# Eight experts in an order ranked on the chip, with weights loaded by register and a kind for 32 tokens

## The chip, the core and the metric

The kernel runs on one core of one Trainium2 chip. The metric is the device time of one execution in microseconds (us), as a median over runs. A profile is one further execution: its span runs from its first instruction to its last.

## The reference

Two layers of a decoder trunk over 256 tokens of width 1024: a token mixer (attention beside a state-space branch), then a channel mixer, which is a dense SwiGLU in layer 0 and eight SwiGLU experts in layer 1. All weights are 32-bit floats. Each token goes to the two experts with the highest router logits:

```python
logits = (t @ w_router + b_router).astype(jnp.float32)
top_val, top_idx = lax.top_k(logits, TOP_K)          # TOP_K = 2 of N_EXPERTS = 8
top_w = jax.nn.softmax(top_val, axis=-1)
gates = jnp.sum(jax.nn.one_hot(top_idx, N_EXPERTS) * top_w[..., None], axis=1)
out = jnp.zeros_like(t)
for e in range(N_EXPERTS):
    out = out + gates[:, e:e + 1] * (jax.nn.silu(t @ w1[e]) * (t @ w3[e])) @ w2[e]
```

The experts' outputs are summed, so their order is free. With the inputs used here the router gives experts 0 to 7 this many tokens: 20, 54, 194, 113, 23, 40, 43, 25. One expert's three matrices (1024 x 2816, twice, and 2816 x 1024) hold 34.6 MB.

## The kernel before

Everything up to the last expert layer stays as it is and is not told here. `moe_begin` (L1078) starts the expert layer while the mixer of layer 1 still runs: it lists the weights of all experts in the order of their use as pieces of 1 MiB (`parts`, L1084: 33 pieces an expert, 22 for the two first matrices and 11 for the last one) and sets up a **ring** of 15 buffers of 1 MiB. `refill` (L178) issues, on SP's DMA queue, the load of the next pieces as far as the ring has room; each load waits for the release of its buffer.

`route` (L1021) computes the logits, the two best experts of a token, the number of tokens of each expert and each token's rank in its expert, and from the counts, on VectorE, a number `ov` for each expert (L1049 to L1051): how many of 64, 128 and 208 the count exceeds. The loop over the experts (L1417) loads that number into a register of all five engines and branches by it (L1426 to L1435). Each expert therefore stands in the program four times, as four **kinds**: `small` for up to 64 tokens, `middle` up to 128, `many` up to 208 and `many` for all 256. Of the four, one runs, and the other three are jumped over. They stand in the program in this order: small, middle, many(208), many(256); small follows the branch directly.

- `small` (L1168) gathers the expert's tokens with a matrix product by a 0/1 matrix (L1175), transposes them (L1183), and runs 11 steps. In a step, `stage1` multiplies the tokens by 512 columns of the first two matrices (L1200), and `stage2` transposes the product of the step before (L1212) and adds its share of the output (L1218). The tokens stand in TensorE as stationary weights of 64 columns; a matrix product is cut into two halves that use two column groups of the array (`tile_position=(0, 64 * h)`) at the same time. The weights come straight from the ring as 32-bit floats. At the end the output is scaled by the gates (L1234) and scattered back over the tokens by another matrix product (L1240), and VectorE adds it to the stream x_t (L1141).
- `middle` (L1245) and `many` (L1316) first split every weight into two parts of a faster format on ScalarE and VectorE (L210, L211) and run three matrix products in place of one.

With the counts above the kinds in order are: small, small, many(208), middle, small, small, small, small. In the tables of the trace "PE" is TensorE, "PEld" its weight loads, DVE VectorE, ACT ScalarE, and a 32-bit matrix product makes two records.

Of the kernel before, what the change touches and what calls it, by code (L numbers as in the profile page):

```python
# [46 lines left out]
MANY = 208  # L47
ENGS = [mybir.EngineType.PE, mybir.EngineType.Activation, mybir.EngineType.DVE, mybir.EngineType.SP,
# [43 lines left out]
def trunk_kernel(ctx: ExitStack, tc: tile.TileContext, xT, sm, co, w_ada0, w_ada, w_in, w_v, s5bc, w_glu,  # L92
# [83 lines left out]
    ring, parts, turn, filled = [], [], [0], [0]  # L176
# [844 lines left out]
    def route(mo, hn, a, sh, b2, xp, lgp, ss, _):  # L1021
# [26 lines left out]
        ov, o64 = tl("ov", [8], I32), lg[:, 0, :]  # L1048
        V.tensor_scalar(o64, ps[:, 16:24], 64.0, None, op0=ALU.is_gt)  # L1049
        V.scalar_tensor_tensor(o64, ps[:, 16:24], float(P), o64, op0=ALU.is_gt, op1=ALU.add)  # L1050
# [8 lines left out]
        return y, rk, ov, (m8, o0, o1)  # L1059
# [18 lines left out]
    def moe_begin():  # L1078
# [6 lines left out]
        for e in range(NE):  # L1085
            for j in range(NB + 1):
                if j < NB:
                    parts.extend((w13m[e, j, :, 4 * i:4 * i + 4, :], 4) for i in range(2))
                if j:
                    parts.append((w2m[e, j - 1], 2))  # L1090
# [7 lines left out]
    def moe():  # L1098
        mo, hn = rt[1]
        sh = rt[0][1]  # L1100
        y0, rk, ov, picks = route(mo, hn, *rt[0])
# [3 lines left out]
        def ahead(e):  # L1105

            if e == 0:
                gates_of(mo, gates, *picks)
            if e < NE - 1:
                slots_of(e + 1)  # L1110
# [5 lines left out]
        def slots_of(e):  # L1116
# [21 lines left out]
        slots_of(0)  # L1138
# [29 lines left out]
        def small(e):  # L1168

            pm = pms[e % 2]  # L1170
            hf = (slice(0, 64), slice(64, 128))
            ps = [mm_ps("xg") for _ in range(2)]
            for tb in range(2):
                for h in range(2):
                    PE.matmul(ps[h][hf[h], :], lhsT=pm[:, tb, 0:64], rhs=hn[:, tb, 512 * h:512 * h + 512],  # L1175
                              start=tb == 0, stop=tb == 1, tile_position=(0, 64 * h))
            xs = mo.tile([P, 512], F32, name=nm("xs"), tag="pt", bufs=2)
            S.activation(xs[hf[0]], ps[0][hf[0], :], AF.Copy)
            V.tensor_copy(xs[hf[1]], ps[1][hf[1], :])
            ps = mm_ps("xg")  # L1180
            xe = lp.tile([P, KC * 64], F32, name=nm("xs"), tag="hh")
            for c in range(4):
                PE.transpose(ps[:, c * P:(c + 1) * P], xs[:, c * P:(c + 1) * P], ident)  # L1183

            xe4, ps4 = (t.rearrange("p (c h s) -> p h c s", c=4, h=2) for t in (xe, ps))
            for h in range(2):
                V.tensor_tensor(xe4[:, h], ps4[:, h], sh[:, 4 * h:4 * h + 4].unsqueeze(2).broadcast_to([P, 4, 64]), op=ALU.add)  # L1187
            y = [ms_ps("y", 0) for _ in range(2)]

            def rows_of(src, rows, cols):  # L1190
                n = min(rows, 2048 // cols)
                return [w[:, r, :] for i in range(0, rows, n)
                        for w in (load_raw(src[:, i:i + n, :], n, cols),) for r in range(n)]

            def stage1(j):
                w = rows_of(w13m[e, j], KC, 512)
                ps = [mm_ps("s1") for _ in range(2)]
                for k in range(KC):
                    for h in range(2):
# [3 lines left out]
                sg = mo.tile([P, 256], F32, name=nm("sg"), tag="pt", bufs=2)  # L1203
# [410 lines left out]
```

## Time and profile before

| what | value |
| --- | --- |
| median of 3 runs (lowest, highest) | 1573.48 us (1571.73, 1580.18) |
| the profiled execution's own time | 1569.24 us |
| its span | 1567.5 us |
| PE busy in the span | 1371.7 us (88%) |
| DVE, ACT, POOL busy | 881.6, 605.2, 318.9 us |
| moved by DMA | 420.37 MB, 268 GB/s over the span |
| chain of waits that ended last | PE 70%, DVE 18%, issue 6% |

The own time is that of the execution with the profile; the span leaves out what lies before the first and after the last instruction. The busy shares are means over stages with different limits: the first 740 us are the two mixers and the dense channel mixer, the rest is the expert layer, and there the share of a single stretch says more than the mean.

### The profile page before, as it was taken

The numbers are of one execution on the slowest core, as the hardware profiler recorded it, in microseconds if no ns is written. First come the engines' busy times: TensorE is split into PE (matmuls) and PEld (weight loads), VectorE is DVE, ScalarE is ACT, GpSimd is POOL, SyncE is SP. The second block draws the span as 40 slices with busy tenths as digits, with TensorE's granted clock in tenths as the row PEclk, the third lists the DMA queues.
The fourth block names the chain that finished last, engine by engine and source line by source line (L and its number), as shares of the span: only waits on it lengthen the run. The fifth ranks groups of instructions, "written<-read, shape, count | busy, mean of one in ns | idle before, by whom it ended". The sixth has DMA issues, their size and how long they took to land.

```text
span 1567.5 us, 24755 instructions
## 1 busy us (share of the span) xinstructions
PE 1371.7 (88%) x9903; PEld 1139.8 (73%) x9903; DVE 881.6 (56%) x1443; ACT 605.2 (39%) x1115; POOL 318.9 (20%) x295
## 2 busy tenths in 40 slices
PE   4788999799998878988998949999799897979796
PEld 3676998699997777988665648988677574747474
DVE  7888679897777778687111036666588301010102
ACT  3453564354455534644111125555477211111112
POOL 0568019986201625050000000000000000000000
PEclk8898999799999899999998969999899998989899
DMA  7454356477776344479899975666399599999993
GB/s 285 174 190 160 125 188 212 136 258 240 261 257 223 133 136 135 166 244 403 359 419 416 419 290 189 215 203 203 130 348 351 212 420 416 419 416 419 417 419 122
DMA packets 60379, 420.37 MB, mean 268 GB/s; under 512 B 6688, under 2 KB 6688, under 8 KB 11296
## 3 DMA queue, kind: packets, MB, share of 16 engines
q1 hardware_dynamic: 56160, 403.34, 67.9%
q0 software_dynamic: 4032, 14.68, 2.8%
q8 instruction: 100, 1.64, 0.4%
q14 instruction: 87, 0.71, 0.1%
HBM read 416.94 MB, written 1.05 MB: 267 GB/s over the span
## 4 chain that ended last, share of the span: by engine, by line
PE 70%; DVE 18%; issue 6%; DMA 2%; ACT 2%; DVEq 0%; SPq 0%; ACTq 0%
PE s L1200 16%; PE mm L231 15%; PE y L1218 8%; DVE wl L211 6%; PE s L1350 4%; PE y L1372 4%; PE facc L971 3%; PE s L1267 3%; PE s L1352 2%; PE y L1286 2%; DMA raw<-in_w13m_dram 2%; DVE acc L309 1%; PE mm L716 1%; PE xg L1175 1%; DVE x_t L1141 1%
## 5 line engine op out<-in xcount | busy, mean ns | idle before, releaser
L211 DVE TENSOR_TENSOR wl<-raw,wh 128x1024 fp32r<-128x1024 f32 (+1 forms) x290 | 391.0, 1363 | 118.6 <-ACT wh L210 116.2
L210 ACT ACTIVATE wh<-raw 128x1024 fp32r<-128x1024 f32 (+1 forms) x290 | 302.3, 1057 | 252.1 <-PE mm L231 102.1
L231 PE MATMUL mm<-hh,wh 128*128 128x256 f32 x864 | 250.7, 292 | 5.1 <-ACT hh L250 2.9
L231 PE MATMUL mm<-hh,wl 128*128 128x256 f32 x864 | 249.7, 290 | 5.8 <-DVE wl L211 5.8
L1200 PE MATMUL s<-raw,xs 128*64 128x256 f32 x1920 | 250.1, 390 | 3.4 <-DVE xs L1187 3.4
L231 PE MATMUL mm<-hl,wh 128*128 128x256 f32 x864 | 249.5, 289 | 2.0 <-DVE hl L251 1.0
L1200 PEld LDWEIGHTS s<-raw,xs 128*64 128x64 f32 x1920 | 183.8, 140 | 48.2 <-issue 13.9
L1205 DVE TENSOR_TENSOR sg<-sg,s 64x256 f32<-64x256 f32 x66 | 28.0, 424 | 318.6 <-ACT sg L1204 269.8
L231 PEld LDWEIGHTS mm<-hh,wl 128*128 128x128 f32 x864 | 169.4, 196 | 9.8 <-DVE wl L211 6.3
L231 PEld LDWEIGHTS mm<-hh,wh 128*128 128x128 f32 x864 | 169.0, 196 | 9.4 <-ACT hh L250 3.3
L231 PEld LDWEIGHTS mm<-hl,wh 128*128 128x128 f32 x864 | 169.2, 196 | 3.7 <-DVE hl L409 1.5
L1218 PE MATMUL y<-raw,gT 128*64 128x512 f32 x520 | 143.1, 600 | 4.7 <-ACT gT L1215 4.7
L1204 ACT ACTIVATE sg<-s 64x256 f32<-64x256 f32 x66 | 24.8, 375 | 314.2 <-PE s L1200 314.2
L1350 PE MATMUL s<-xe,wh 128*128 128x416 f32 x352 | 107.2, 368 | 2.0 <-DVE sg L1360 1.7
L1352 PE MATMUL s<-xe,wl 128*128 128x208 f32 x352 | 91.0, 258 | 0.0
L309 DVE SCALAR_TENSOR_TENSOR acc<-raw,cond,acc 128x512 f32<-128x512 f32 x91 | 81.4, 894 | 1.6
L1218 PEld LDWEIGHTS y<-raw,gT 128*64 128x64 f32 x520 | 51.1, 136 | 40.9 <-issue 30.5
L317 POOL TENSOR_TENSOR araw<-araw,cond 128x1024 f32<-128x1024 f32 x28 | 62.3, 2229 | 71.8 <-DMA araw<-in_w_ada_dram 71.8
L1350 PEld LDWEIGHTS s<-xe,wh 128*128 128x128 f32 x352 | 66.2, 188 | 4.3 <-DVE sg L1360 2.4
L1352 PEld LDWEIGHTS s<-xe,wl 128*128 128x128 f32 x352 | 67.3, 191 | 0.4
L971 PE MATMUL facc<-fgh,wh 128*128 128x256 f32 x352 | 62.9, 281 | 0.2 <-ACT wh L210 0.2
L321 POOL TENSOR_TENSOR araw<-araw,araw 128x1024 f32<-128x1024 f32 x21 | 58.2, 2773 | 1.6
(513 smaller groups left out, 2369.0 us busy)
## 6 DMA issues: line engine op xcount, KB each, us to landing
raw<-in_w13m_dram SPq DMA_DIRECT2D x160, 1024.0 KB, 13.8
raw<-in_w2m_dram SPq DMA_DIRECT2D x87, 1024.0 KB, 13.7
raw<-in_w_ada_dram SPq DMA_DIRECT2D x32, 1024.0 KB, 5.1
raw<-in_w_in_dram SPq DMA_DIRECT2D x28, 1024.0 KB, 5.0
raw<-in_w13d_dram SPq DMA_DIRECT2D x22, 1024.0 KB, 5.0
late<-in_w13m_dram SPq DMA_DIRECT2D x16, 1024.0 KB, 16.2
araw<-in_w_ada_dram POOLq DMA_DIRECT2D x28, 512.0 KB, 4.6
raw<-in_w2d_dram SPq DMA_DIRECT2D x11, 1024.0 KB, 5.0
```

Source lines behind the costliest of these rows:

```text
L210: S.activation(hv, rv, AF.Copy)
L211: V.tensor_tensor(lv, rv, hv.bitcast(F32), op=ALU.subtract)
L231: PE.matmul(ps, lhsT=a[k][:, c0:c0 + P], rhs=b[:, k, :], start=k == 0 and i == 0 and o % 2 == 0, stop=k == n - 1 and i == 2 and o % 2 == 1)
L309: V.scalar_tensor_tensor(acc0, raw[:, k, :], c, acc0, op0=ALU.mult, op1=ALU.add)
L317: G.tensor_tensor(raw, raw, cond[:, r0:r0 + 2].unsqueeze(2).broadcast_to([P, 2, 512]), op=ALU.mult)
L321: G.tensor_tensor(acc, acc, raw, op=ALU.add)
L971: PE.matmul(o, lhsT=a[k][:, oc * P:(oc + 1) * P], rhs=b[:, k, :], start=j == 0 and oc % 2 == 0 and k == 0 and i == 0, stop=j == NB - 1 and ...
L1200: PE.matmul(ps[h][hf[h], 0:256], lhsT=xe4[:, k // 4, k % 4, :], rhs=w[k][:, 256 * h:256 * h + 256], start=k == 0, stop=k == KC - 1, tile_p ...
L1218: PE.matmul(y[h][hf[h], :], lhsT=g[:, k, :], rhs=w[k][:, 512 * h:512 * h + 512], start=j == 0 and k == 0, stop=j == NB - 1 and k == 1, til ...
L1350: PE.matmul(ps[:, 0:2 * nb], lhsT=hs[k][:, c], rhs=x.rearrange("p i s -> p (i s)"), start=k == 0, stop=False)
L1352: PE.matmul(ps[:, nb:2 * nb], lhsT=ls[k][:, c], rhs=x[:, 0, :], start=False, stop=k == KC - 1)
L1372: PE.matmul(y[b][n][0:s1 - s0, :], lhsT=g[:, k, s0:s1], rhs=w[w_][k][:, n * 512:n * 512 + 512], start=j == 0 and k == 0 and i == 0, stop=j ...
```

## The change

Expert 0 stays first. Experts 1 to 7 are ranked by their number of tokens on the chip (`ordered`), and position i of 1 to 7 gets the expert of rank PLACE[i-1], rank 0 having most tokens. `place` is a new row of constants; `bring` picks a row's values into the new order by a sum over a 0/1 matrix. The ranks `rk`, the gates and the kinds are brought into this order, and the expert of each position is loaded into a register of SP, from which the addresses of its weights are made. `small` takes its number of rows n as an argument (32 or 64), and cuts each product into 128/n column groups; its two halves' results now share one PSUM tile. The branches are nested so that the heavy kinds follow directly and the small ones are jumped to.

With the counts above positions 0 to 7 hold experts 0, 2, 7, 3, 5, 1, 6, 4, and their kinds are small(32), many(208), small(32), middle, small(64), small(64), small(64), small(32).

```diff
+PLACE = (0, 5, 1, 4, 2, 3, 6)
     def refill():
         while filled[0] < min(len(parts), turn[0] + len(ring)):
-            src, rows = parts[filled[0]]
+            w, e, (j, i), rows = parts[filled[0]]
+            if e and not experts:
+                return
+            src = w[0, j] if e == 0 else w[bass.ds(experts[e - 1], 1), j].squeeze(0)
+            if i is not None:
+                src = src[:, 4 * i:4 * i + 4, :]
...
-        V.tensor_scalar(o64, ps[:, 16:24], 64.0, None, op0=ALU.is_gt)
-        V.scalar_tensor_tensor(o64, ps[:, 16:24], float(P), o64, op0=ALU.is_gt, op1=ALU.add)
+        V.tensor_scalar(o64, ps[:, 16:24], 32.0, None, op0=ALU.is_gt)
+        for n in (64, P):
+            V.scalar_tensor_tensor(o64, ps[:, 16:24], float(n), o64, op0=ALU.is_gt, op1=ALU.add)
+        key = tl("key", [8])
+        V.scalar_tensor_tensor(key, ps[:, 16:24], 8.0, cov('iota8'), op0=ALU.mult, op1=ALU.subtract)
+    def ordered(mo, key, ov, rk):
+        above, rank, ow, seq = tl("above", [8, 8]), tl("rank", [8]), tl("ow", [8, 8]), tl("seq", [2, 8])
+        V.tensor_tensor(above[:, 0:7, 0:7], key[:, 1:8].unsqueeze(1).broadcast_to([P, 7, 7]),
+                        key[:, 1:8].unsqueeze(2).broadcast_to([P, 7, 7]), op=ALU.is_gt)
+        V.memset(rank[:, 0:1], -1.0)
+        V.reduce_sum(rank[:, 1:8], above[:, 0:7, 0:7], axis=AX.X)
+        V.tensor_tensor(ow, rank.unsqueeze(1).broadcast_to([P, 8, 8]), cov('place').unsqueeze(2).broadcast_to([P, 8, 8]),
+                        op=ALU.is_equal)
+        def bring(o, row):
+            V.tensor_tensor(above, ow, row.unsqueeze(1).broadcast_to([P, 8, 8]), op=ALU.mult)
+            V.reduce_sum(o, above, axis=AX.X)
+        bring(seq[:, 0, :], cov('iota8'))
+        bring(seq[:, 1, :], ov)
+        si = tl("si", [2, 8], I32)
+        V.tensor_copy(si, seq)
+        for tb in range(2):
+            bring(seq[:, tb, :], rk[:, tb, :])
+        return bring, si, seq
...
+        for e in range(1, NE):
+            experts.append(nc.values_load(si[0:1, 0, e:e + 1], engines=[mybir.EngineType.SP], min_val=0, max_val=NE - 1,
...
-        def small(e):
+        def small(e, n):
+            G_ = P // n
+            cb = KC // G_
+            gr = [slice(n * g, n * g + n) for g in range(G_)]
...
+                c_ = 512 // G_
                 for k in range(KC):
-                    for h in range(2):
-                        PE.matmul(ps[h][hf[h], 0:256], lhsT=xe4[:, k // 4, k % 4, :], rhs=w[k][:, 256 * h:256 * h + 256],
-                                  start=k == 0, stop=k == KC - 1, tile_position=(0, 64 * h))
+                    for g in range(G_):
+                        PE.matmul(ps[gr[g], 0:c_], lhsT=xe4[:, k // cb, k % cb, :], rhs=w[k][:, c_ * g:c_ * g + c_],
+                                  start=k == 0, stop=k == KC - 1, tile_position=(0, n * g))
...
-            for h in range(2):
-                S.activation(ys[hf[h]], y[h][hf[h], :], AF.Copy, scale=gs[hf[h]])
+            S.activation(ys, y[:, 0:w_], AF.Copy, scale=gs)
...
-            rv = nc.values_load(ov[0:1, e:e + 1], engines=ENGS, min_val=0, max_val=3,
+            rv = nc.values_load(si[0:1, 1, e:e + 1], engines=ENGS, min_val=0, max_val=4,
...
-            with tc.If(rv < 1) as c:
-                arm(small)
+            with tc.If(rv < 2, preferred_fallthrough_block=False) as c:
+                with tc.If(rv < 1, preferred_fallthrough_block=False) as c1:
+                    arm(lambda e: small(e, 32))
+                with c1.Else():
+                    arm(lambda e: small(e, 64))
             with c.Else():
-                with tc.If(rv < 2) as c2:
+                with tc.If(rv < 3, preferred_fallthrough_block=False) as c2:
                     arm(middle)
                 with c2.Else():
-                    with tc.If(rv < 3) as c3:
+                    with tc.If(rv < 4) as c3:
                         arm(lambda e: many(e, MANY))
```

Three places show how instructions move (a number behind a name is that of the buffer).

**TensorE at the second position: which kind follows the branch.** Before, the branch rows of the second position, each with the first row behind it (L1175 is `small`, L1254 `middle`, L1333 `many`):

```order
L1418 TENSOR_LOAD rov_7908
L1426 COMPARE_AND_BRANCH
L1175 MATMUL xg_12670<-late,pm_7921 64x512
...
L1426 UNCONDITIONAL_BRANCH
L1429 COMPARE_AND_BRANCH
L1254 MATMUL xg_13096<-pm_7921,late 128x128 x8
...
L1429 UNCONDITIONAL_BRANCH
L1432 COMPARE_AND_BRANCH
L1333 MATMUL xg_13981<-pm_7921,late 128x128 x2
```

Now (L1382 is `many`, L1223 `small`, with 64 rows first and with 32 rows behind it, L1303 `middle`):

```order
L1467 TENSOR_LOAD rsi_7939
L1476 COMPARE_AND_BRANCH
L1482 COMPARE_AND_BRANCH
L1485 COMPARE_AND_BRANCH
L1382 MATMUL xg_15304<-pm_7924,late 128x128 x2
...
L1485 UNCONDITIONAL_BRANCH
L1477 COMPARE_AND_BRANCH
L1223 MATMUL xg_14007<-late,pm_7924 64x512 x4
...
L1477 UNCONDITIONAL_BRANCH
L1223 MATMUL xg_13376<-late,pm_7924 32x256 x8
...
L1477 UNCONDITIONAL_BRANCH
L1303 MATMUL xg_14419<-pm_7924,late 128x128 x8
```

Where `small` followed its branch directly, `many` for 208 tokens now does. A small(64) is reached by one taken branch (over `many`), a small(32) by two (over `many`, then over small(64)), a `middle` by one. Each kind but the last in the program ends with a branch behind all of them, before and now.

**TensorE in one step of the kind for 32 rows** (L1250 is `stage1`, L1263 the transpose and L1268 the product of `stage2`):

```order
L1263 MATMUL gT_13598<-co_t,sg_13544 128x64
L1250 MATMUL s_1952_13611<-late,xe_13389 32x128 x5
L1268 MATMUL y_13396<-raw_7663,gT_13600 32x256 x8
L1250 MATMUL s_1952_13611<-late,xe_13389 32x128 x11
L1250 MATMUL s_1952_13611<-raw_7650,xe_13389 32x128 x16
```

A step has 32 products of 128 columns and 8 of 256, where `small` before has 16 of 256 and 4 of 512: twice as many, half as long, and four of them side by side in the array where two were.

**VectorE between the counts and the branch's value.** These rows stand between the last comparison of the counts (L1059) and the load of the kind (L1467):

```order
L1059 SCALAR_TENSOR_TENSOR rov_7908<-rank_7902,rlg_7885 128x8
L1062 TENSOR_TENSOR rrk_7913<-rank_7902,roh_7898 128x16
L1065 SCALAR_TENSOR_TENSOR rkey_7916<-rank_7902,co_t 128x8
L1063 TENSOR_SCALAR rrk_7913<-rrk_7913 128x16
L1079 TENSOR_TENSOR rabove_7927<-rkey_7916 128x7x7
L1158 TENSOR_SCALAR pm_7923<-co_t,rrk_7913 128x128 x2
L1082 TENSOR_REDUCE rrank_7928<-rabove_7927 128x7
L1084 TENSOR_TENSOR row_7929<-rrank_7928,co_t 128x64
L1088 TENSOR_TENSOR rabove_7927<-row_7929,co_t 128x64
L1089 TENSOR_REDUCE rseq_7930<-rabove_7927 128x8
L1088 TENSOR_TENSOR rabove_7927<-row_7929,rov_7908 128x64
```

One more sum (L1089) and the cast to whole numbers (L1093) follow, and then the branch's value is there; before, L1051 gave it directly.

## Rows read from the trace of the kernel before

**Rows 1.** Window: busy us of PE, PEld, DVE, ACT, POOL; granted clock, DMA share, GB/s.

```profile
1396.00:1479.00 83.00, 73.44 (x510) 48.12 (x508) 9.63 (x23) 9.51 (x26) 0.00 (x0) 0.93 1.01 418
```

**Rows 2.** Timeline of PE, one step: start us, us, engine, line, operation, tiles, shapes, count.

```profile
1455.18 0.34 PE L1212 MATMUL gT<-co_t,sg 64*128 64x64 f32 x2
1457.72 3.18 PE L1200 MATMUL s<-raw,xs 128*64 128x256 f32 x26
1460.84 0.34 PE L1212 MATMUL gT<-co_t,sg 64*128 64x64 f32 x2
```

**Rows 3.** Timeline of PE, a small expert's first and last products; idle time before in brackets.

```profile
1394.20 3.68 PE L1175 MATMUL xg<-late,pm 128*64 128x512 f32 x8 [5.95 <-issue]
1466.93 3.22 PE L1240 MATMUL sc<-ge,ys 64*128 64x256 f32 x16 [0.77 <-ACT ys L1234]
1476.51 3.68 PE L1175 MATMUL xg<-late,pm 128*64 128x512 f32 x8 [6.35 <-issue]
```

**Rows 4.** Timeline of PE, sixteen narrow products; then their line's row, ns min/median/max.

```profile
499.18 0.54 PE L672 MATMUL kps<-vt,bp 128*32 128x96 f32 x16
L672 PE MATMUL kps<-vt,bp x128: 245/246/271, 156.1 to 501.0; 128*32 128x96 f32 x128
```

**Rows 5.** DMA issues of 1 MiB: count, KB, median us from issue to landing.

```profile
raw<-in_w13d_dram SPq DMA_DIRECT2D x22, 1024.0 KB, 5.0
```

**Rows 6.** Refill at a start: SP's DMA issue; busy time by window (as rows 1).

```profile
1239.96 0.33 SPq L183 DMA_DIRECT2D raw<-in_w13m_dram  x1
1233.00:1239.00 6.00, 4.55 (x22) 1.77 (x20) 1.45 (x3) 0.59 (x1) 0.00 (x0) 0.77 0.00 0
```

**Rows 7.** Timeline of PE and ACT, end of the last expert.

```profile
1546.38 1.94 PE L1218 MATMUL y<-raw,gT 128*64 128x512 f32 x8 [0.43 <-ACT gT L1215]
1548.34 1.39 ACT L1234 ACTIVATE ys<-y,gs 64x512 f32<-64x512 f32 x2 [2.02 <-PE y L1218]
```

**Rows 8.** Timeline, first row of a kind, idle time before it in brackets; last row DVE.

```profile
924.14 1.19 PE L1333 MATMUL xg<-pm,late 128*128 128x128 f32 x4 [20.70 <-issue]
1117.75 6.37 PE L1254 MATMUL xg<-pm,late 128*128 128x128 f32 x32 [6.87 <-DVE wl L211]
1232.22 3.60 PE L1175 MATMUL xg<-late,pm 128*64 128x512 f32 x8 [3.63 <-issue]
917.74 0.48 DVE L1119 TENSOR_SCALAR pm<-co_t,rrk 128x128 f32<-128x128 f32 x2 [13.42 <-issue]
```

**Rows 9.** PE's branches: line, queue, count, ns min/median/max, start us.

```profile
L1426 PEldq COMPARE_BRANCH  x1: 95/95/95, 744.4 to 744.4; - x1
L1426 PEldq COMPARE_BRANCH  x1: 6138/6138/6138, 820.5 to 820.5; - x1
L1426 PEldq COMPARE_BRANCH  x1: 7179/7179/7179, 909.1 to 909.1; - x1
L1429 PEldq COMPARE_BRANCH  x1: 7396/7396/7396, 916.5 to 916.5; - x1
L1426 PEldq COMPARE_BRANCH  x1: 4356/4356/4356, 1113.1 to 1113.1; - x1
L1429 PEldq COMPARE_BRANCH  x1: 3958/3958/3958, 1227.5 to 1227.5; - x1
```

**Rows 10.** Busy time by window around branches (columns as rows 1).

```profile
744.00:752.00 8.00, 4.84 (x16) 1.79 (x18) 5.19 (x28) 1.87 (x2) 0.00 (x0) 0.71 0.94 388
902.00:924.00 22.00, 1.32 (x8) 0.64 (x6) 4.49 (x12) 2.95 (x3) 0.00 (x0) 0.56 0.97 382
1107.00:1117.00 10.00, 3.87 (x30) 3.67 (x30) 7.40 (x15) 4.79 (x6) 0.00 (x0) 0.79 0.04 8
1227.00:1232.00 5.00, 1.59 (x14) 1.38 (x12) 3.70 (x9) 0.00 (x0) 0.00 (x0) 1.00 0.03 7
```

**Rows 11.** Timeline of DVE and PE at the start of the experts.

```profile
743.35 0.17 DVE L1051 SCALAR_TENSOR_TENSOR rov<-rank,rlg 128x8 int32<-128x8 f32 x1
744.69 3.39 PE L1175 MATMUL xg<-late,pm 128*64 128x512 f32 x8 [1.77 <-DMA raw<-in_w13m_dram]
```

More of the change, by code (lines that the diff above doesn't have):

```diff
@@ L173, in wtile @@
             i -= b
-    ring, parts, turn, filled = [], [], [0], [0]
+    ring, parts, experts, turn, filled = [], [], [], [0], [0]
     def refill():
         while filled[0] < min(len(parts), turn[0] + len(ring)):
-            src, rows = parts[filled[0]]
+            w, e, (j, i), rows = parts[filled[0]]
[4 more added lines that the diff above has]
+                src = src[:, 4 * i:4 * i + 4, :]
             b = ring[filled[0] % len(ring)].rearrange("p (r c) -> p r c", r=rows)
@@ L1087, in moe_begin @@
                 if j < NB:
-                    parts.extend((w13m[e, j, :, 4 * i:4 * i + 4, :], 4) for i in range(2))
+                    parts.extend((w13m, e, (j, i), 4) for i in range(2))
                 if j:
-                    parts.append((w2m[e, j - 1], 2))
+                    parts.append((w2m, e, (j - 1, None), 2))
         ring.extend([rp.tile([P, 2048], F32, name=nm("raw"), tag="raw", bufs=MR) for _ in range(MR)])
@@ L1100, in moe @@
         sh = rt[0][1]
-        y0, rk, ov, picks = route(mo, hn, *rt[0])
+        y0, rk0, ov, key, picks = route(mo, hn, *rt[0])
         gates = mo.tile([P, 2, 8], F32, name="gates")
@@ L1108, in ahead, with slots_of @@
                 gates_of(mo, gates, *picks)
+                for tb in range(2):
+                    bring(gates[:, tb, :], gates[:, tb, :])
             if e < NE - 1:
-                slots_of(e + 1)
+                slots_of(e + 1, rk)
         gt2 = ada_v(1, 5)
         pms = [mo.tile([P, 2, P], F32, name=f"pm{i}") for i in range(2)]
-        def slots_of(e):
+        def slots_of(e, rk):
             for tb in range(2):
@@ L1136, in back_of @@
             return ge, gs
-        slots_of(0)
+        slots_of(0, rk0)
+        bring, si, rk = ordered(mo, key, ov, rk0)
+        for e in range(1, NE):
+            experts.append(nc.values_load(si[0:1, 0, e:e + 1], engines=[mybir.EngineType.SP], min_val=0, max_val=NE - 1,
+                                          skip_runtime_bounds_check_because="it is a sum over a one-hot row"))
         def add_back(e, ch, y):
@@ L1188, in small @@
-            y = [ms_ps("y", 0) for _ in range(2)]
+            xe4, ps4 = (t[:, 0:KC * n].rearrange("p (c g s) -> p g c s", c=cb, g=G_) for t in (xe, ps))
+            for g in range(G_):
+                V.tensor_tensor(xe4[:, g], ps4[:, g], sh[:, cb * g:cb * g + cb].unsqueeze(2).broadcast_to([P, cb, n]),
+                                op=ALU.add)
+            y = ms_ps("y", 0)
             def rows_of(src, rows, cols):
-                n = min(rows, 2048 // cols)
-                return [w[:, r, :] for i in range(0, rows, n)
-                        for w in (load_raw(src[:, i:i + n, :], n, cols),) for r in range(n)]
+                m = min(rows, 2048 // cols)
+                return [w[:, r, :] for i in range(0, rows, m)
+                        for w in (load_raw(src[:, i:i + m, :], m, cols),) for r in range(m)]
@@ L1417, in moe @@
         for e in range(NE):
-            rv = nc.values_load(ov[0:1, e:e + 1], engines=ENGS, min_val=0, max_val=3,
-                                skip_runtime_bounds_check_because="it is a sum of three comparisons")
+            rv = nc.values_load(si[0:1, 1, e:e + 1], engines=ENGS, min_val=0, max_val=4,
+                                skip_runtime_bounds_check_because="it is a sum of four comparisons")
             def arm(f):
@@ L1561, in pack @@
     puc('iota8', np.broadcast_to(np.arange(8, dtype=f32)[None], (P, 8)))
+    puc('place', np.broadcast_to(np.array((-1,) + PLACE, dtype=f32)[None], (P, 8)))
     puc('iota128', np.broadcast_to(np.arange(P, dtype=f32)[None], (P, P)))
```

75 lines of the change are left out of this document (37 added, 38 removed).

## The prediction

> **What bounds the kernel now.** I read the busy time by window first. Over one period of a light expert near the end, PE is busy for 73 of 83 us while the DMA engines are at a share of 1.01 and move 418 GB/s [rows 1]: both are near their limit. 1 MiB at 418 GB/s is 2.51 us, so the 33 blocks of an expert need 82.8 us. The timeline of PE says which of the two leads. Between two transposes of `stage2` lie 1460.84 - 1455.18 = 5.66 us, one of eleven steps, with no row that waits for a DMA [rows 2]. A step takes three blocks, 7.53 us of DMA; the ring of 15 blocks pays the difference, and is filled again in the idle time between the experts, so it is not PE that waits. A light expert is bound by PE: from its first product (1394.20) to the end of its last (1466.93 + 3.22 = 1470.15) it takes 75.95 us, and then PE idles for 6.35 us until the next [rows 3]. That idle time is the second thing to read: 3.63 to 6.87 us ahead of most experts, but 20.70 us ahead of the third [rows 8]. PE's branch records fill it: a branch that is not taken lasts 95 ns, a taken one 4 to 7.4 us [rows 9].
>
> **The kind for 32 tokens.** It runs at positions 0, 2 and 7. The nearest row for its products: sixteen records of 96 columns with 32-wide weights, spread over four column groups by L672, take 0.54 us, and one alone 0.246 us [rows 4], so one adds (0.54 - 0.246)/15 = 20 ns. With two groups, 26 records of 256 columns take 3.18 us [rows 2], about 0.38 us for the first and 112 ns for each further one; that is 224 ns for 256 columns on one group, or 84 ns for 96. The 20 ns are a quarter of it: four groups do work at once. So each group's columns are halved, and of a step's 5.66 us the products, some 5 us, shrink to 2.5: a step of about 3.2 us. [...] The expert's time follows from the ring. Before, SP issued its first refill 1239.96 - 1232.22 = 7.7 us after the first product, and DMA stood still until then [rows 6]; with shorter first products I take 5.7 to 6.1 us. A block lands 5.0 us after an issue on an empty queue [rows 5], and block 33 is the 18th to be fetched: 6 + 5 + 17 x 2.51 = 53.6 us. Behind it come its products (1.3), the scaling (0.4) and the scatter (3.2, as in rows 3), 4.9 us: 58.5 us instead of 75.95. Two such experts give -34.9. The last one ends with the work that follows it: its last product of `stage2` ended at 1546.38 + 1.94 = 1548.32 of a span of 1567.5 [rows 7], 19.2 us ahead of the end. Before, from 1476.51 to the end, 91.0 us; now 53.6 + 1.3 + 0.2 + 18.9 = 74.0: -17.0. Bounds for each: 62 (a release later by 3 us) and 55 (the first block of the next expert issued earlier).
>
> **The kind for 64 tokens** keeps its products; at its end one operation on ACT replaces two that took 1.39 us [rows 7], -0.7 each, three times -2.1. `many` and `middle` are unchanged but for their place, 0; both take longer than 82.8 us, so a ring that a light expert left empty fills beside them. That is the cover of this zero: if it fails, `middle` waits for its first blocks, at most 5.0 us.
>
> Experts together: **-34.9 - 17.0 - 2.1 = -54.0 us**.
>
> **The jumps between experts.** Every kind ends with one taken branch, before and now. What changes are the branches ahead of a kind: before 0 for `small`, 1 for `middle`, 2 for `many`; now 0 for `many`, 1 for small(64) and `middle`, 2 for small(32). Prices: the first, at the end of an expert, is in the gaps (5.95 to 6.35 in rows 3, a record of 6.14 in rows 9, with the DMA engines full). One further jump cost 7.18 and 7.40 us with DMA at 0.97, and 4.36 and 3.96 where DMA was at 0.04 and 0.03 [rows 9, 10]; I take 7.3 and 4.2. Which price holds is read from the kind that ends: `many` and `middle` leave the ring full and DMA still; the light kinds leave blocks queued (33 released in 75 us, at most 30 landed). In order:
>
> - 0 to 1 (`many`): 6.1, as before.
> - 1 to 2 (small(32)), behind `many`: 6.87 with two taken [rows 8], one more, 11.0.
> - 2 to 3 (`middle`): 5.95 + 7.3 = 13.3.
> - 3 to 4 (small(64)), behind `middle`: 3.63 [rows 8] + 4.2 = 7.8.
> - 4 to 5 and 5 to 6: 13.3 each.
> - 6 to 7 (small(32)): three taken, as in the 20.70 of before, 20.7.
>
> Sum 85.5. Before, in order: 6.1 + 20.7 + 6.87 + 3.63 + 5.95 + 5.95 + 6.35 = 55.5 (rows 3 and 8; one 5.95 stands for two). **+30.0 us**.
>
> [...]
>
> **The start.** Before, the branch's value was there at 743.35 + 0.17 = 743.52 and the first product ran at 744.69 [rows 11]. Now a dozen operations on VectorE stand ahead of it, each 0.17 to 0.28 us: +2.6 at the end of the chain. Then two jumps ahead of small(32) on PE, while DMA is still at 0.94 [rows 10]: 6.0 and, the ring being full by then, 4.2. First product at 757.5 instead of 744.7: **+12.8**, between +7 (both jumps hidden behind the chain in part) and +17.5 (both full price). SP also loads seven registers and adds one operation per DMA. No row shows that; the nearest is SP's spacing of issues, 2.51 us each, so I take 0, and up to 1 us for the loads.
>
> **Sum against the profiled execution**: -54.0 + 30.0 + 12.8 = -11.2, its own time 1569.24 becomes 1558.0; the median shown is 4.2 us above that execution, so 1562. The prices move it: with 62 or 55 us for a small(32) it is +10 or -10, so the likeliest case alone spans 1552 to 1572.
>
> **Rivals.**
>
> *B, jumps at the low price.* An extra jump costs what it does without DMA traffic, 4 us, and a first one 3.63. For it: behind `middle` the ring is full, and light experts with longer gaps need blocks at less than the rate that DMA has (75 + 13 = 88 us against 82.8). Against it: at the end of each light expert some 7 blocks are still queued: 33 are released, and 65/2.51 = 26 land, since the first takes 10 us. Gaps 7 x 3.63 + 8 x 4.2 = 59, +3.5; start +10.8; sum -39.7: 1534.
>
> *C, jumps at the full price everywhere, slower.* Let q be the price of every further jump. Eight of them stand between experts and one more at the start; with 5.95 for each first one the growth is 9q - 5.2. At q = 7.3 it is 60.5, net +6.5, 1580; at 8.0, near the 13.42 us that VectorE idled over two jumps and more [rows 8], net +12.8, 1586. It decides for slower than the old time from q = 6.6. For it: all seven prices measured while DMA was full are 6 to 7.4. Against it: behind `many` and `middle` DMA stands at 0.03 and 0.04 [rows 10].
>
> [...]
>
> *E, the kind for 32 does not gain*, because its four groups run one behind the other: a step would take 10.2 us, PE would lead, and each of three experts would take 11 x 4.5 = 50 us more than before: 150 - 2 + 43 more in all, 1764. Rows 4 all but exclude it.
>
> **How the numbers follow.** The likeliest case 0.50, B 0.20, C 0.20, D 0.03, E 0.02, 0.05 for mishaps of either sign. About 0.5% of the time, 7.9 us, is what a measurement can tell from no change: faster means below 1565.6, slower above 1581.3. Of the likeliest case (1552 to 1572) about 0.55 lies below 1565.6 and the rest within; B and D are faster; of C half is within, half slower: 0.28 + 0.20 + 0.03 and a little = 0.53; slower 0.10 + 0.02 + 0.03 of mishaps = 0.15; within 0.32. The range takes in B's lower edge and C: 1530 to 1586.
>
> **What would show it.** In the new profile: small(32) with PE rows that wait for `raw<-in_w13m_dram`, 57 to 60 us long, DMA share about 1 from its sixth us on; small(64) 75 us; the idle time ahead of `many` 6 us, ahead of the last expert 20 us, ahead of small(64) 13 us behind a light one and 8 behind `middle`; branch records at 7 us or 4 us by the DMA share beside them; the first product at 757. The prediction is wrong if a small(32) takes over 62 us (then PE or the release leads), if small(64) stays at 6 us of idle time (jumps are cheap, B or D), or if jumps behind `middle` cost 7 us (C).

## The result

| kernel | median us (lowest, highest; runs) | ratio to before, 95% interval |
| --- | --- | --- |
| before | 1572.67 (1564.14, 1583.30; 14) | 1 |
| the change | 1584.01 (1573.88, 1588.97; 14) | 1.0058 [1.0034, 1.0081] |

The change is slower by some 0.6%, 11 us between the medians; 1562 us, 10 us faster, was forecast. Its profiled execution took 1586.95 us, with a span of 1585.2 us, 17.7 above that of before. Two executions that took far longer, 1984 us of the kernel before and 4953 us of the version with the likely kind first (below), stand in no ratio.

The timeline of PE of the changed kernel shows the first product of each position with the idle time before it (the seventh position, left out, is like the sixth at 1323.17):

```profile
767.10 1.93 PE L1223 MATMUL xg<-late,pm 128*32 128x256 f32 x16 [15.59 <-DVE rw L428]
...
835.74 1.20 PE L1382 MATMUL xg<-pm,late 128*128 128x128 f32 x4 [5.89 <-issue]
...
1036.02 1.93 PE L1223 MATMUL xg<-late,pm 128*32 128x256 f32 x16 [9.23 <-DVE pm L1158]
...
1111.51 5.71 PE L1303 MATMUL xg<-pm,late 128*128 128x128 f32 x32 [12.80 <-issue]
...
1234.73 3.68 PE L1223 MATMUL xg<-late,pm 128*64 128x512 f32 x8 [7.66 <-issue]
...
1323.17 3.68 PE L1223 MATMUL xg<-late,pm 128*64 128x512 f32 x8 [13.50 <-issue]
...
1507.64 1.94 PE L1223 MATMUL xg<-late,pm 128*32 128x256 f32 x16 [21.01 <-issue]
```

Against [rows 3, 8]: the 20.70 us ahead of `many` are 5.89 now, and small(64) and the last expert have 13.5 and 21.0 where `small` had 6. The branch records of PE behind it, by line (columns as rows 9; five single branches of L1476, then three of L1477):

```profile
L1476 PEldq COMPARE_BRANCH  x1: 6602/6602/6602, 755.6 to 755.6; - x1
L1476 PEldq COMPARE_BRANCH  x1: 4287/4287/4287, 1026.7 to 1026.7; - x1
L1476 PEldq COMPARE_BRANCH  x1: 4457/4457/4457, 1230.0 to 1230.0; - x1
L1476 PEldq COMPARE_BRANCH  x1: 7317/7317/7317, 1404.1 to 1404.1; - x1
L1476 PEldq COMPARE_BRANCH  x1: 7526/7526/7526, 1492.5 to 1492.5; - x1
L1477 PEldq COMPARE_BRANCH  x1: 4641/4641/4641, 762.3 to 762.3; - x1
L1477 PEldq COMPARE_BRANCH  x1: 4805/4805/4805, 1031.1 to 1031.1; - x1
L1477 PEldq COMPARE_BRANCH  x1: 7396/7396/7396, 1500.1 to 1500.1; - x1
```

The windows of the changed kernel (columns as rows 1) give the DMA share ahead of the seventh, the last and the third position, and then three stretches of the first small(32):

```profile
1398.00:1411.00 13.00, 0.31 (x2) 0.00 (x0) 1.12 (x3) 0.00 (x0) 0.00 (x0) 0.66 1.01 394
1486.00:1507.00 21.00, 0.64 (x4) 0.23 (x2) 1.45 (x4) 0.00 (x0) 0.00 (x0) 0.54 0.97 375
1027.00:1036.00 9.00, 0.00 (x0) 0.01 (x1) 1.19 (x4) 0.00 (x0) 0.00 (x0) 0.68 0.05 10
...
780.00:790.00 10.00, 9.73 (x244) 7.13 (x235) 0.87 (x3) 1.48 (x6) 0.00 (x0) 1.00 0.99 410
810.00:820.00 10.00, 5.67 (x117) 3.73 (x113) 0.31 (x2) 0.76 (x3) 0.00 (x0) 0.84 1.01 419
820.00:826.00 6.00, 4.51 (x37) 1.83 (x41) 0.27 (x1) 0.70 (x2) 0.00 (x0) 0.50 1.03 425
```

A taken branch ahead of a kind cost 7.3 to 7.5 us at a DMA share of 0.97 to 1.01 and 4.3 to 4.8 us at 0.05 (behind `many` and `middle`). Of small(32), PE is the limit in the first steps (busy 9.73 of 10 us) and DMA later (5.67 of 10); at its end the granted clock is 0.50.

All of the difference, by stretches of PE's timeline, in us against before; the second column of measurements is another profile of the same kernel, below:

| term | forecast | first profile | second profile |
| --- | --- | --- | --- |
| everything up to the counts (742.9 before) | 0 | +8.6 | -1.4 |
| idle time ahead of the first product (1.77 before) | +12.8 | +13.8 | +14.1 |
| five light experts (378.7 before) | -37.0 | -28.2 | -25.9 |
| last expert to the end (91.0 before) | -17.0 | -13.4 | -10.8 |
| `many` (186.7 before) | 0 | +4.3 | +3.1 |
| `middle` (110.8 before) | 0 | +4.7 | +4.9 |
| idle time between experts (55.5 before) | +30.0 | +27.9 | +29.5 |
| sum | -11.2 | +17.7 | +13.5 |

The first row is no work of the change: in the profiles of all kernels here it lies between 738.7 and 757.4 us.

### The profile page after: what moved, and what is told of

The parts are those of the page before. It is cut to its first block, busy times and chain, and to the rows that moved or that the text cites. A ratio compares the mean times of both kernels' runs of the same rounds, so it can differ in the third digit from the quotient of the medians.

```text
span 1585.2 us, 27912 instructions
## 1 busy us (share of the span) xinstructions
PE 1312.7 (83%) x11256; PEld 1118.8 (71%) x11256; DVE 877.4 (55%) x1468; ACT 594.5 (38%) x1109; POOL 319.5 (20%) x295
## 4 chain that ended last, share of the span: by engine, by line
PE 64%; DVE 18%; issue 9%; DMA 5%; ACT 2%; DVEq 0%; ACTq 0%; SPq 0%
PE mm L238 17%; PE s L1250 10%; DVE wl L218 5%; PE y L1268 5%; PE s L1399 4%; PE y L1421 4%; DMA raw<-in_w2m_dram 4%; PE facc L978 3%; PE s L1316 3%; PE s L1401 2%; PE y L1335 2%; DVE acc L316 2%; PE mm L723 2%; DMA raw<-in_w13m_dram 1%; PE xg L1223 1%
## 5 line engine op out<-in xcount | busy, mean ns | idle before, releaser
L1250 PE MATMUL s<-raw,xe 128*32 128x128 f32 (+1 forms) x2880 | 203.6, 328 | 15.1 <-DMA raw<-in_w13m_dram 10.0
L1250 PEld LDWEIGHTS s<-raw,xe 128*32 128x32 f32 (+1 forms) x2880 | 159.9, 125 | 42.9 <-DMA raw<-in_w13m_dram 14.3
L1255 DVE TENSOR_TENSOR sg<-sg,s 64x256 f32<-64x256 f32 (+1 forms) x66 | 23.6, 358 | 293.9 <-ACT sg L1254 293.9
L1254 ACT ACTIVATE sg<-s 64x256 f32<-64x256 f32 (+1 forms) x66 | 21.3, 323 | 268.2 <-PE s L1250 268.2
L1268 PE MATMUL y<-raw,gT 128*32 128x256 f32 (+1 forms) x784 | 110.9, 478 | 9.1 <-DMA raw<-in_w2m_dram 4.3
L1223 PE MATMUL xg<-late,pm 128*32 128x256 f32 (+1 forms) x72 | 16.8, 778 | 80.4 <-issue 55.6
L1268 PEld LDWEIGHTS y<-raw,gT 128*32 128x32 f32 (+1 forms) x784 | 44.3, 122 | 36.0 <-issue 12.6
L1223 PEld LDWEIGHTS xg<-late,pm 128*32 128x32 f32 (+1 forms) x72 | 4.6, 178 | 86.7 <-issue 86.7
```

Source lines behind the costliest of these rows:

```text
L1250: PE.matmul(ps[gr[g], 0:c_], lhsT=xe4[:, k // cb, k % cb, :], rhs=w[k][:, c_ * g:c_ * g + c_], start=k == 0, stop=k == KC - 1, tile_positi ...
L1268: PE.matmul(y[gr[h], 0:w_], lhsT=g[:, k, :], rhs=w[k][:, w_ * h:w_ * h + w_], start=j == 0 and k == 0, stop=j == NB - 1 and k == 1, tile_p ...
```

## Experiments

**Each position's likely kind first.** If taken branches took the gain, a version without them must have it.

```diff
+FIRST = (0, 3, 0, 2, 1, 1, 1, 0)
-            with tc.If(rv < 2, preferred_fallthrough_block=False) as c:
-                with tc.If(rv < 1, preferred_fallthrough_block=False) as c1:
+            with tc.If(rv < 2, preferred_fallthrough_block=FIRST[e] < 2) as c:
+                with tc.If(rv < 1, preferred_fallthrough_block=FIRST[e] < 1) as c1:
...
-                with tc.If(rv < 3, preferred_fallthrough_block=False) as c2:
+                with tc.If(rv < 3, preferred_fallthrough_block=FIRST[e] < 3) as c2:
```

> The change, but each position of the program puts another kind directly behind its branch: small(32) at positions 0, 2 and 7, many at 1, middle at 3, small(64) at 4 to 6. With these counts no taken branch stands ahead of any kind; the ten of the change fall away, those that end a kind stay. Theory 1 (the change loses its gain to taken branches, at the gaps that its trace shows): start -11, ahead of position 2 -6, of 3 -12, of 4 -4, of 5 and 6 -7 each, of 7 -15, together -62 or about 1522 us; shorter gaps make DMA the limit of the last four experts, which gives back some 5, so 1520 to 1535. Theory 2 (the loss is the ranking, the loads by register and small(32) waiting for DMA; branches are hidden by other work): within 10 us of the change, 1574 to 1590.

Measured: 1532.84 us, 0.9729 [0.9661, 0.9796], and 1532.68 us, 0.9745 [0.9724, 0.9767], in a second measurement: 51 us below the change, 39 below before. Its timeline of PE at the third, fourth, sixth and last position:

```profile
1006.33 1.91 PE L1224 MATMUL xg<-late,pm 128*32 128x256 f32 x16 [2.25 <-issue]
...
1073.05 6.21 PE L1304 MATMUL xg<-pm,late 128*128 128x128 f32 x32 [6.41 <-issue]
...
1268.49 3.68 PE L1224 MATMUL xg<-late,pm 128*64 128x512 f32 x8 [6.12 <-issue]
...
1434.04 1.93 PE L1224 MATMUL xg<-late,pm 128*32 128x256 f32 x16 [6.28 <-issue]
```

9.2, 12.8, 13.5 and 21.0 us became 2.3, 6.4, 6.1 and 6.3. As foreseen a part comes back: the last expert takes 1520.7 - 1434.04 = 86.7 us in place of 77.6, since with shorter pauses DMA leads: in a second profile of this version PE waits 10.6 us for blocks at the last expert, in the change 4.5. Theory 1 holds. This is the version to keep, for counts that fall as here; with other counts the program takes other branches and pays for them (none were run).

**Small kinds first everywhere.**

```diff
-            with tc.If(rv < 2, preferred_fallthrough_block=False) as c:
-                with tc.If(rv < 1, preferred_fallthrough_block=False) as c1:
+            with tc.If(rv < 2, preferred_fallthrough_block=True) as c:
+                with tc.If(rv < 1, preferred_fallthrough_block=True) as c1:
```

> The change with the nesting turned round at every position: small(32) directly behind the branch, then small(64), then middle, then many. Six taken branches ahead of kinds in place of ten. Theory 1: start -11 (no taken branch), ahead of many +15 (two taken while DMA is full, as the 20.7 us before the change), ahead of position 2 -6, of 7 -15, the others as they are: -17, about 1567 us. Theory 2: no difference beyond 5 us, 1579 to 1589.

Measured: 1567.71 us, 0.9962 [0.9927, 0.9998], as theory 1 says. Its timeline of PE ahead of `many`, `middle` and the last expert:

```profile
821.46 1.19 PE L1382 MATMUL xg<-pm,late 128*128 128x128 f32 x4 [12.48 <-issue]
...
1095.40 5.45 PE L1303 MATMUL xg<-pm,late 128*128 128x128 f32 x32 [20.82 <-DVE pm L1158]
...
1473.12 1.93 PE L1223 MATMUL xg<-late,pm 128*32 128x256 f32 x16 [6.14 <-issue]
```

Two single terms were off, though not their sum: in this nesting `many` still stands ahead of `middle`, so it is reached with one taken branch fewer than I had counted, and `middle`, with one more, pays 20.8 in place of 12.8.

**The nesting alone, on the kernel before.**

```diff
-            with tc.If(rv < 1) as c:
+            with tc.If(rv < 1, preferred_fallthrough_block=False) as c:
...
-                with tc.If(rv < 2) as c2:
+                with tc.If(rv < 2, preferred_fallthrough_block=False) as c2:
```

> The kernel before with only the nesting of the change: many directly behind the branch, middle and small jumped to; no ranking, no kind for 32, weights by fixed addresses. Ahead of many two taken branches fewer, ahead of each of the six small ones one more. Theory 1: -15 ahead of many, +5 at the start, +4 behind middle, +7.4 at each of four others: +24, about 1597 us. Theory 2 (branches are hidden): 1568 to 1578 us.

Measured: 1603.09 us, 1.0173 [1.0118, 1.0228]. Of the timeline of PE, `many` and a later `small`:

```profile
933.75 1.20 PE L1333 MATMUL xg<-pm,late 128*128 128x128 f32 x4 [6.12 <-issue]
...
1337.21 3.68 PE L1175 MATMUL xg<-late,pm 128*64 128x512 f32 x8 [13.53 <-DVE pm L1119]
```

The nesting by itself costs 27 us by the ratio, 32 between the medians: `many` gains 14.6, and six light experts lose 4 to 8 each.

**The kind for 32 taken out.**

```diff
-                    arm(lambda e: small(e, 32))
+                    arm(lambda e: small(e, 64))
```

> The change with small(64) in the place of small(32), reached by the same branches; order, ranking, loads by register and number of taken branches stay. Theory 1 (small(32) gives what its trace shows, 62.7 us against 74.9 and 77.6 against 91.0): +12 twice and +13, 1616 to 1626 us. Rival (small(32) gives nothing, since what it finishes early is waited for again by the next expert's first weights): 1580 to 1595.

Measured: 1616.39 us, 1.0280 [1.0205, 1.0355]. The kind for 32 is worth 32 us. The three experts took 76.86, 74.94 and 90.1 us, where the change has 62.75, 62.69 and 77.6: what it finishes early is not waited for again by the next expert's first weights. But it is not free for the kind behind it: here `many` and `middle` take 186.8 and 110.4 us, as before (186.7 and 110.8), and behind a small(32), with the same branches, 191.1 and 115.6. The last part comes back to this.

**Order and registers**, both on the version with the likely kind first. Fixed addresses:

```diff
...
-            src = w[0, j] if e == 0 else w[bass.ds(experts[e - 1], 1), j].squeeze(0)
+            src = w[ORDER[e], j]
...
```

> The version with each position's likely kind directly behind its branch (1532.8 us), with the seven registers of SP and the addresses made from them taken out: the weights are loaded in the order 0, 2, 7, 3, 5, 1, 6, 4 by fixed addresses, so the order holds for these inputs only. Theory 1 (SP has 2.5 us for each issue, loads by register cost nothing): 1525 to 1540. Rival (SP's later or slower issues delay the refill): 10 us or more below 1533.

Measured: 1536.13 us, 0.9760 [0.9711, 0.9808]: no difference from 1532.8, so the loads by register cost nothing that shows. The experts' own order:

```diff
-FIRST = (0, 3, 0, 2, 1, 1, 1, 0)
+FIRST = (0, 1, 3, 2, 0, 1, 1, 0)
...
-            src = w[0, j] if e == 0 else w[bass.ds(experts[e - 1], 1), j].squeeze(0)
+            src = w[e, j]
...
-        bring, si, rk = ordered(mo, key, ov, rk0)
+        si, rk = mo.tile([P, 2, 8], I32, name="si"), rk0
+        V.tensor_copy(si[:, 1, :], ov)
...
```

> The same version without ranking: experts in their own order 0 to 7, weights by fixed addresses, the kind for 32 tokens kept, and each position's likely kind (small(32), small(64), many, middle, small(32), small(64), small(64), small(32)) directly behind its branch. Theory 1: the last four experts are limited by DMA in both orders (132 blocks, 15 of them in the ring, about 330 us), so the order is worth only what position 1 loses, small(64) at 75 to 77 us in place of a small(32) at 62, less 3 us for the chain on VectorE: 1538 to 1548. Rival (the order is what makes small(32) pay): 1555 or more.

Measured: 1546.11 us, 0.9830 [0.9784, 0.9875]. The order is worth some 13 us, net of its chain on VectorE, a quarter of what the branches are.

**What sets a branch's price.** The change, with SP held back at a light expert:

```diff
-        while filled[0] < min(len(parts), turn[0] + len(ring)):
+        while filled[0] < min(cap[0], turn[0] + len(ring)):
...
             V.tensor_copy(xs[hi], ps[hi, 0:w_])
+            if e:
+                nc.sync.dma_start(dum, xs[0:1, 0:8])
+                refill()
...
```

`cap` is 33 blocks times the experts begun, so no block is loaded ahead of its expert; a heavy kind refills the ring as it begins.

> The change, with the loads of a light expert's first weights held back until its tokens are gathered (SP waits for a small copy from the gathered tokens; nothing is left out), so that the DMA engines stand still during the branches ahead of it. It is slower for it, some 1690 us, as the ring starts empty at each light expert. To be read are the branch records of TensorE at positions 4 to 7: if a taken branch waits for a fetch that shares the DMA engines with the weights, the 7.3 to 7.5 us records of L1476 and L1477 become 3.5 to 4.8 us, as behind many and middle; if the price is that of the distance jumped, they stay at 7.

Measured: 1677.4 us, one run. Its branch records at the sixth and seventh position, by line:

```profile
L1486 PEldq COMPARE_BRANCH  x1: 4737/4737/4737, 1349.7 to 1349.7; - x1
L1486 PEldq COMPARE_BRANCH  x1: 4577/4577/4577, 1451.6 to 1451.6; - x1
```

The window around the second one, columns as rows 1:

```profile
1448.00:1458.00 10.00, 1.58 (x5) 0.58 (x6) 1.32 (x5) 0.00 (x0) 0.00 (x0) 0.65 0.05 11
```

And the timeline of PE, sixth and last position:

```profile
1354.73 3.68 PE L1225 MATMUL xg<-late,pm 128*64 128x512 f32 x8 [8.46 <-DVE pm L1158]
...
1563.64 1.93 PE L1225 MATMUL xg<-late,pm 128*32 128x256 f32 x16 [12.84 <-issue]
```

The same branches over the same distance fell from 7.3 to 7.5 us to 4.6 to 4.7, the gaps from 13.5 to 8.5 and from 21.0 to 12.8. So about 4.6 us are the branch's own and some 2.8 us the weights' traffic beside it. What a branch waits for in its own 4.6 us no run shows: the change's trace lists two DMA queues of the kind `instruction`, with 253 packets and 3.08 MB (187 and 2.35 MB before), but no row ties a branch to them, and the fetch named in the expectation was my supposition.

**A second profile of the change**, unaltered.

> The change once more, unaltered, for a second profile. In its first one many took 191.1 us (186.7 before), middle 115.6 (110.8), small(32) 62.7 (58.5 foreseen), and the mixers ahead of the experts were 8.7 us longer than before. Theory 1 (only small(32) is mis-sized; the rest scatters from execution to execution): small(32) 62 to 64 again, many back at 187, the mixers anywhere within 10 us. Rival (the ring that a light expert leaves empty slows the heavy one behind it): many 191 and middle 115 again.

Measured: 1588.13 us, 1.0103 [1.0058, 1.0148]; the terms are in the table. `middle` is 115.73 us again, `many` 189.80, and only the first row of the table comes back to the time of before. The rival is nearer, though not for its reason, as the last part shows.

**The end of small(32) at a higher clock.** On the version with the likely kind first:

```diff
+                if n == 32 and j > 4:
+                    pd = mm_ps("pd")
+                    for k in range(KC):
+                        for g in range(G_):
+                            PE.matmul(pd[gr[g], 0:c_], lhsT=xe4[:, k // cb, k % cb, :], rhs=w[7][:, c_ * g:c_ * g + c_],
+                                      start=k == 0, stop=k == KC - 1, tile_position=(0, n * g))
```

> The version with each position's likely kind directly behind its branch; in small(32), from the sixth step on, stage1's 32 products by its last rows are issued once more into a PSUM tile that nobody reads, so that TensorE idles less while it waits for weights (nothing of the result changes). In the change's trace the granted clock is 0.50 in the last 16 us of small(32) and 0.68 in the first 10 us of many behind it, and 6.7 us pass from the last landed block to the last product, where 4.9 were foreseen. Theory 1 (the low clock makes these 1.8 us): the clock stays near 1.0, 4.9 us, small(32) 60 to 61 us in place of 63, and up to 2 us less in the kind behind it; in the time 3 to 10 us less than the same version without it. Rival (the products only delay the release of blocks and the end): small(32) 63 us or longer, no gain.

> The version with each position's likely kind directly behind its branch once more, beside the run with the added products on the same chip: 1525 to 1540 us, small(32) at position 0 near 63 us, the granted clock at its end near 0.5.

Measured: 1554.77 us, 0.9891 [0.9864, 0.9919], beside 1532.68 without: 22 us slower. The first small(32) took 76.29 us (64.51 without). Its timeline of PE, from the steps with added products:

```profile
779.17 1.14 PE L1257 MATMUL pd<-raw,xe 128*32 128x128 f32 x33 [1.83 <-issue]
...
785.35 1.72 PE L1257 MATMUL pd<-raw,xe 128*32 128x128 f32 x50 [1.44 <-issue]
...
791.49 0.30 PE L1251 MATMUL s<-raw,xe 128*32 128x128 f32 x2 [1.26 <-issue]
```

And the window from the first of these stops to the second, columns as rows 1:

```profile
779.17:785.35 6.18, 4.74 (x128) 3.77 (x128) 0.29 (x1) 0.49 (x2) 0.00 (x0) 1.00 1.01 415
```

My expectation fell. (Its first reading was off as well: the clock is 0.50 in the last 10 us of the change's first small(32), and 0.64 over the last 16.) PE stops every 6.2 us for nothing that the profile shows, in the middle of a group of products. From one stop to the next lie 128 products and 128 weight loads; the eight stops of this small(32) come 254 to 256 records apart (not 245, as I write below). The change has such stops too, but few: in its first small(32) one of 1.08 us at 790.80 and, 254 records behind it, one of 0.37 us at 797.23. A stop that comes by the count of records looked like the instruction stream, so the same work was put into fewer instructions:

```diff
-                    for k in range(KC):
-                        for g in range(G_):
-                            PE.matmul(pd[gr[g], 0:c_], lhsT=xe4[:, k // cb, k % cb, :], rhs=w[7][:, c_ * g:c_ * g + c_],
-                                      start=k == 0, stop=k == KC - 1, tile_position=(0, n * g))
+                    for k in range(2):
+                        PE.matmul(pd[gr[0], 0:512], lhsT=xe4[:, k // cb, k % cb, :], rhs=w[7],
+                                  start=k == 0, stop=k == 1, tile_position=(0, 0))
```

> As the version with added products, but the added work of a step (about 1.7 us of TensorE, read by nobody) is 2 products of 512 columns on one column group in place of 32 of 128 columns on four: the same time on the array with a sixteenth of the instructions. In the version before, small(32) took 76.3 and 68.4 us, and PE stood for 1 to 1.8 us, waiting for nothing the profile shows, every 6.2 us or about 245 records of PE and its weight loads. Theory A (TensorE's instruction stream, fetched beside the weights, was the limit): these gaps go, small(32) is 60 to 64 us, and the time 1525 to 1540. Theory B (the added work itself delays blocks and end): small(32) stays at 68 to 76 us and the time at 1550 to 1560. The granted clock at the end of small(32) is read too: near 1.0 with a tail of 4.9 us if idle time had lowered it, else 0.5.

Measured: 1533.58 us, 0.9750 [0.9697, 0.9804], small(32) 64.24 and 61.39 us: theory A. Of eight stops in the first small(32) one is left, of 0.33 us, and of seven in the second two, of 1.1 us, about as many as without added products. The added work of a step was as long, 1.88 us of PE in 4 records where 64 records took 1.99, so the number of instructions makes the stops; that PE waits there for instructions fetched beside the weights, as theory A has it, no run shows. The end of its first small(32) in the timeline of PE:

```profile
815.60 1.07 PE L1274 MATMUL y<-raw,gT 128*32 128x256 f32 x16 [1.08 <-DMA raw<-in_w2m_dram]
...
818.55 2.39 PE L1295 MATMUL sc<-ge,ys 32*128 32x256 f32 x8 [0.56 <-DVE x_t L1186]
```

The window ahead of its end:

```profile
814.00:819.00 5.00, 2.75 (x39) 1.19 (x31) 0.98 (x3) 0.47 (x1) 0.00 (x0) 1.00 1.02 421
```

The clock stays at 1.00 to here, and from the first product by the last block to the end pass 820.94 - 815.60 = 5.3 us in place of the change's 6.7. That the added products hold the clock up is not shown: the version without them had 1.00 there as well in one of its two profiles (rows in the last part). The last block's products came 58.9 us behind the first product, and 58.5 without the added ones (56.0 in the change: without the jumps PE waits 4.4 us for VectorE's copy of the first tokens, 1.0 in the change). Nothing is gained in all.

## Why the prediction was wrong

The forecast came out on the wrong side by its steps for the kinds, not by that for the branches.

**Branches: right.** Forecast for the seven gaps 6.1, 11.0, 13.3, 7.8, 13.3, 13.3, 20.7; measured 5.9, 9.2, 12.8, 7.7, 13.5, 13.4, 21.0. The two prices, read from the DMA share beside the branches, held, and the run with DMA held back shows that the traffic makes the difference between them. The start (+13.8 for +12.8) held as well, and its parts: without the jumps, chain and branch took 4.5 us in place of 15.6 (of the 11 us, 3.3 come back there in the wait for VectorE told above).

**Small(32): right in kind, mis-sized.** "6 + 5 + 17 x 2.51 = 53.6 us" and "4.9 us" behind it, 58.5 in all, measured 62.75 and 62.69 (61.57 and 63.06 in the second profile). The rows of the changed kernel's first one, SP's first refill:

```profile
773.51 0.34 SPq L190 DMA_DIRECT2D raw<-in_w13m_dram  x1
```

and PE's last product of `stage2` and last scatter:

```profile
823.12 1.94 PE L1268 MATMUL y<-raw,gT 128*32 128x256 f32 x16 [0.55 <-DMA raw<-in_w2m_dram]
...
827.46 2.39 PE L1289 MATMUL sc<-ge,ys 32*128 32x256 f32 x8 [0.56 <-DVE x_t L1185]
```

The refill began at 6.4 us, the last block's products at 823.12, 56.0 us behind the first product, and 6.7 us went by from there to the end. So 0.4 us belong to the refill, 1.8 to the tail and 2.0 to the blocks.

The tail is the clock's. It ran at a granted clock of 0.50 (window 820 to 826 above); in the first profile of the version with the likely kind first the same products ran at 1.00 and took 808.70 + 1.87 - 805.75 = 4.8 us, as forecast (the last row is a window of that stretch, columns as rows 1):

```profile
805.75 1.07 PE L1269 MATMUL y<-raw,gT 128*32 128x256 f32 x16 [1.41 <-DMA raw<-in_w2m_dram]
...
808.70 1.87 PE L1290 MATMUL sc<-ge,ys 32*128 32x256 f32 x8 [0.56 <-DVE x_t L1186]
...
803.00:810.57 7.57, 4.93 (x49) 2.55 (x49) 2.41 (x7) 0.70 (x2) 0.00 (x0) 1.00 1.01 417
```

The blocks I had counted at 2.51 us each from the first landing on. In the changed kernel's trace they land in the order of their issue, the first 5.2 us behind its issue, the second and third 3.3 and 3.8 us after the one ahead, and each of the other fifteen some 2.5 us after it. Its windows from the first issue to the third landing and from there to the eighteenth (columns as rows 1):

```profile
773.51:785.83 12.32, 12.32 (x315) 10.38 (x311) 1.32 (x5) 2.13 (x8) 0.00 (x0) 0.97 0.90 342
785.83:822.99 37.16, 26.86 (x558) 17.83 (x550) 2.04 (x7) 3.68 (x15) 0.00 (x0) 0.89 1.01 421
```

In the first window some 4.2 MB were moved, and three blocks are 3.1 MB: about one block's worth belonged to blocks further back in the queue. The queue lost its 2 us while it filled, and then kept to 2.5 us a block.

At the last expert 3.6 us are missing too (6.2 in the second profile). Together these are 12 us of the 22 by which the median was missed. The bound that I had given, 62, was nearer. Over 62 us was also my sign that PE or the release leads; it came, but DMA led.

**Heavy kinds: "unchanged but for their place, 0" failed.** They make 9 and 8 us of the difference in the two profiles. `middle` took 4.7 and 4.9 us more. The cover that I named, the ring, held: PE waited for no block there. It waited for VectorE. VectorE's first operation of `middle`:

```profile
1116.76 0.48 DVE L1158 TENSOR_SCALAR pm<-co_t,rseq 128x128 f32<-128x128 f32 x2 [17.53 <-issue]
```

and PE's wait behind its first products:

```profile
1120.17 0.71 PE L1166 MATMUL gt<-co_t,pm 128*128 128x128 f32 x4 [2.96 <-DVE xt L1306]
```

VectorE stood for 17.5 us over its branches where PE stood for 12.8 (18.0 and 12.6 in the second profile, where the wait is 3.85 us). I had read the 13.42 us in [rows 8] and then priced PE alone. In the version with the likely kind first VectorE stands for 9.9 us there, PE for 6.4, and `middle` takes 113.0; with the kind for 32 taken out, over the same branches, VectorE stands for 12.2, PE for 13.7, there is no such wait, and `middle` takes 110.4. Why VectorE needs longer behind small(32) than behind small(64) was not tried. What the wait leaves, 1.8 and 1.0 us, lies beside a lower clock: the second 10 us of `middle`, before and then now (columns as rows 1):

```profile
1127.75:1137.75 10.00, 9.89 (x45) 7.66 (x44) 9.20 (x10) 8.16 (x10) 0.00 (x0) 1.00 0.91 329
1121.51:1131.51 10.00, 9.65 (x36) 7.70 (x36) 7.94 (x11) 6.34 (x8) 0.00 (x0) 0.83 1.01 414
```

`many` took 4.3 us more in one profile and 3.1 in the other, almost all of it in two places, its first products (10.9 and 11.1 us in place of 9.5) and its last ones. The granted clock is lower in both. The first 10 us, before and then now:

```profile
924.14:934.14 10.00, 10.00 (x69) 10.00 (x70) 5.09 (x8) 2.60 (x4) 0.00 (x0) 0.78 0.48 168
835.74:845.74 10.00, 9.69 (x58) 9.39 (x59) 5.86 (x12) 2.29 (x4) 0.00 (x0) 0.67 1.01 417
```

Its last group of products, in the changed kernel:

```profile
1020.03 6.77 PE L1461 MATMUL sc<-gel,ys 128*128 128x256 f32 x30 [0.28 <-DVE ys L1451]
```

and in the version with the likely kind first:

```profile
1000.21 3.87 PE L1462 MATMUL sc<-gel,ys 128*128 128x256 f32 x30 [0.28 <-DVE ys L1452]
```

Same instructions: 3.86 or 3.87 us before and in five other profiles, 5.3 to 5.4 in four, 6.75 to 6.77 in three, where the granted clock is lower (0.66 from 1017 to 1027 us in the first of these two, 1.00 from 996 to 1004 us in the other). The version with the likely kind first had 3.87 us in one profile and 6.77 in its other, so this changes from execution to execution. But it goes with the kind ahead: of the nine profiles with a small(32) ahead of `many` seven have the longer group, of the four with 64 rows ahead (before, the nesting alone, the kind for 32 taken out, the experts' own order) none. So a light expert that leaves PE waiting for DMA may well lower the clock for the kind behind it; no run changes the clock alone, and this stays open.

**Rival C** gave nearly the measured time (1580) for the wrong reason: behind `many` and `middle` the branches stayed at 4.3 to 4.8 us. That 1584 lies within 1530 to 1586 is owed to C's edge alone, and so is luck; the case that I held likeliest ended at 1572. B and D, with further jumps at 4 and at 0.1 us, are out by the branches of 7.3 to 7.5 us, E too (small(32) does gain 13 us).

## What to carry to other kernels

Before a tuned block is put behind a branch, count taken branches on the path of the engine that sets the end, and on every engine that it waits for, and price each by the DMA share beside it: here ten of them cost 51 us, more than the 32 us that the faster kind gained. Where a program is unrolled, each place can have its own likely kind directly behind its branch; that turned +0.6% into about -2.6%. When a bound by transfers replaces a bound by an engine, take the time of the last block from a run in which such a queue fills, price the tail at the clock that the waiting engine is left with (0.50 here), and do not put the kinds behind it at nothing: `many` and `middle` paid 9 us for a faster neighbour.

## What the runs showed of the hardware

- A taken branch on PE ahead of a kind took 4.3 to 4.8 us at a DMA share of 0.05 to 0.08, 6.6 us at 0.68 and 7.0 to 7.5 us at 0.97 to 1.01, by the same code; one not taken took 0.06 to 0.10 us.
- Over the same two taken branches VectorE stood for 17.5 and 18.0 us where PE stood for 12.8 and 12.6.
- Straight code lost time by its number of instructions: with narrow products beside a DMA share of 1.01 to 1.02, PE stopped for 0.5 to 2.3 us after every 254 to 256 records of products and weight loads; with a sixteenth of the added instructions for the same work, one to three stops were left of seven or eight. What PE waits for in such a stop no run shows.
- The same 30 products at the end of `many` took 3.87, 5.3 to 5.4 or 6.77 us in different executions, with the granted clock (1.00 for the first, 0.66 for the last).
